# A cosine attention kernel: five score banks, wide exponentials, norms in the value banks and joint sums

## The chip, the cores and the metric

The kernel runs on one core of a Trainium2 chip. The metric is the device time of one execution in microseconds (us); lower is better. Five engines of the core work side by side, each through its own list of instructions in order: PE (matrix products), ACT (exponentials and other functions), DVE (vector work), POOL (vector work on the SBUF alone) and SP, which here only issues transfers. They wait for one another on semaphores.

## The reference

```python
Q_norm = Q / (np.linalg.norm(Q, axis=-1, keepdims=True) + 1e-10)
K_norm = K / (np.linalg.norm(K, axis=-1, keepdims=True) + 1e-10)
scores = np.einsum('bhqd,bhkd->bhqk', Q_norm, K_norm) / tau
weights = np.exp(scores - np.max(scores, axis=-1, keepdims=True))
weights = weights / (np.sum(weights, axis=-1, keepdims=True) + 1e-10)
return np.einsum('bhqk,bhkd->bhqd', weights, V).astype(np.float32)
```

Batch 8, 12 heads, sequence 512, width 64, tau 0.1, all in f32. Normalised scores are bounded, so the kernel takes no maximum.

## The kernel before, in words

The 96 heads are taken as 48 pairs (numbered 0 to 47; `s` in the code). A pair passes through these steps:

- **Load** (SP): Q, K and V of two heads, 256 KB each, into rings of buffers: `qk` (17 deep), `vf` (8). Each output goes out the same way from `ob` (8 deep), so the normalisation of pair s waits for the store of pair s-8.
- **Squares** (POOL, L368) into `sq`; **sums of squares**: K's on PE, as eight matmuls with the identity (`SSQ`, L385) that leave eight partial sums in columns 320 to 383 of a value bank, which DVE reduces (`RED`, L392); Q's by DVE straight from the SBUF (L396).
- **Norms**: eight small steps on DVE (`NEW`, L419 to L430), an inverse square root by a bit trick and two refinements, for a group of one, two or four pairs at a time. Its working values stand in `n_ps`, a PSUM bank of its own.
- **Scaling** to bf16 (`SCL`, L451): Q on DVE, K on POOL for most pairs. **Transposes** on PE (`TR`, L457), copied out by DVE (`EVA`, L465) into `qt`.
- **Scores** on PE (`SCO`, L551): a pair has eight tiles of 128 keys by 512 queries (four key blocks `c` by two heads `h`). One step of scores makes the two heads' tiles of a key block, in two of the four banks of `sc_ps`. The two heads lie in different halves of the rows.
- **Exponentials** on ACT (`EXP`, L567): one instruction of 1024 columns for both tiles, into `et` (five pairs deep). The next step of scores into these two banks waits for it. Pair 0 is done tile by tile (L543), the last block of pair 47 in three pieces (L562), and one block of pair 43 is done by a polynomial on DVE and POOL.
- **Values** on PE (`PV`, L587): sixteen matmuls for each head, into bank 0 or 1 of `o_ps`; then a reciprocal (`RCP`, L599) and a normalisation (`NRM`, L604) on DVE. A bank's next user waits for the normalisation, or for the reduction of the sums put there in between (`attached`).

Nothing is scheduled while it runs. `ORDER`, a table of numbers, sets each engine's list by hand, and the waits follow from each step's `needs`. Waits between two steps of PE, or of ACT, are left out, since those run in order.

The code picks the two banks for a key block's scores by turns:

```python
turn = chunks.index((s, c))
b = turn % 2
...
used = ... exps(*chunks[turn - 2])
P.add(("SCO", s, c), "pe", "sco", T0 + 0.9 * c, [("EVA", s)] + used, sco)
```

Of the kernel before, what the change touches and what calls it, by code (L numbers as in the profile page):

```python
# [108 lines left out]
def bass_cosine_similarity_attention_kernel(  # L109
# [26 lines left out]
    et = [sb(f"et{i}", [128, NT, 2, SEQ], bf16) for i in range(R_ET)]  # L136
# [13 lines left out]
    xw = sb("xw", [128, 2, SEQ], f32)  # L150

    sc_ps = nc.alloc_psum_tensor("scps", [128, 4, SEQ], f32)
# [5 lines left out]
    n_ps = nc.alloc_psum_tensor("nps", [128, R_X, MOST], f32)  # L158
# [34 lines left out]

    P.add("one", "pool", "one", -100, [], lambda e: e.memset(ones[:, :], 1.0))
# [23 lines left out]
    slots = sorted((START + PERIOD * (s + 1) + 0.9 * PV_AT[4 * h + 3] + 0.05 + late(s), s, h) for s in range(NP - 1) for h in range(2))  # L218
    chunks = [(s, c) for s in range(NP) for c in range(NT) if (s, c) not in OFF]
    off_of = {s: c for s, c in OFF}  # L220
    poly_groups = {group[s] for s in off_of}
# [4 lines left out]
    session, attached, early = {}, {}, []  # L226
    for s, w in sorted(((s, w) for s in range(NP) for w in range(2) if on_pe(s, w)), key=lambda j: (due_red(j[0]), j)):
        at = due_red(s) + 0.3
        if s < EARLY:
            early.append((s, w))  # L230
            continue
        due, i, h = next(x for x in slots if x[0] >= at and (x[1], x[2]) not in attached)
        attached[i, h] = (s, w)
        session[s, w] = (h, due, [("PV", i, h, NT - 1)])
    before = [[("EVA", 0, 1, 0), ("EVA", 0, 1, 1)], []]
    for s, w in sorted(early):
        b = w if s >= ONE_BANK else 0
        session[s, w] = (b, due_red(s), before[b])
        before[b] = [("RED", s, w)]
    bank_free = {}  # L240
    for s in range(NP):
        for h in range(2):
            bank_free[s, h] = before[h]
            before[h] = [("NRM", s, h)] + ([("RED",) + attached[s, h]] if (s, h) in attached else [])

    def head0(TF):
        for h in range(2):
# [10 lines left out]
            r_ps = sc_ps[:, 1, 0:4] if h == 0 else n_ps[:, 0, 0:4]  # L258
# [68 lines left out]

    def pair(s):
# [20 lines left out]
        red = [[("RED", 0, w, 0), ("RED", 0, w, 1)] if s == R_SQ else [key("RED", s - R_SQ, w)] for w in range(2)]  # L349
# [27 lines left out]
        for w in range(2):  # L377
            sqs = squares(s, w)
# [19 lines left out]
        xg, tg, yg = xs[g % R_X][:, 0 : 2 * m], ts[g % R_X][:, 0 : 2 * m], n_ps[:, g % R_X, 0 : 2 * m]  # L398
# [4 lines left out]
        reds = [("RED", i, w) for i in range(first[g], first[g] + sizes[g]) for w in range(2)]  # L403
# [14 lines left out]
        elif s == first[g]:  # L418
# [17 lines left out]
            for k in news(g):  # L436
                needs = [done] if k else reds + [("SCL", i, w) for i in past for w in range(2) if w == 0 or i in K_ON_DVE]
                if k == 0 and g == R_X:
# [3 lines left out]
                done = ("NEW", g, k)  # L442
                P.add(done, "dve", "new7" if k == 7 and on_dve else "new", TF - 4.9 - slack(s, M_NEW) + (M_STEP * (k - 7) if s > 8 else 0.23 * k), needs, steps[k])

        for w in range(2):
# [4 lines left out]
                  [("NEW", g, root(s, w))] + ([("TR", 0, w, 0), ("TR", 0, w, 1)] if s == R_QN else [key("TR", s - R_QN, w)]),  # L450
# [19 lines left out]
    def scos(s):  # L470
        if s < 0:
            return []
        if s in off_of:
            return [("SCO", s, c) if c != off_of[s] else ("SCX", s, c - c) for c in range(NT)] + [("SCX", s, 1)]
        return [("SCO", s, c) for c in range(NT)] if s else [("SCO", 0, c, h) for c in range(NT) for h in range(2)]

    def last_step(s, c):
        return 4

    def exps(s, c):  # L480
        if s < 0:
            return []
        if s == NP - 1 and c == NT - 1:
            return [("EXP", s, c, k) for k in range(3)]
        if s == 0:
            return [("EXP", s, c, h) for h in range(2)]
        return [("Y", s, last_step(s, c)) if (s, c) in OFF else ("EXP", s, c)]

    def poly(s, c, at):
# [3 lines left out]
        xp, xz = xps[len(prev) % 2], xzs[len(prev) % 2]  # L493
        done = lambda k: [("Y", prev[-k], last_step(prev[-k], off_of[prev[-k]]))] if len(prev) >= k else []
        a0, a1, a2, a3 = POLY
        for h in range(2):
            users = turn_user[turns[h]]
            before = [("X",) + users[users.index((s, h)) - 1] + (1,)] if users.index((s, h)) else []

            def sco(e, h=h):  # L500
                return e.matmul(out=x_ps, lhsT=qt[s % R_QT][64 * h : 64 * h + 64, 1, c, :],
                                rhs=qt[s % R_QT][64 * h : 64 * h + 64, 0, :, :], start=True, stop=True)

            P.add(("SCX", s, h), "pe", "sco1", at + h, [("EVA", s), ("EVA", turns[h])] + before, sco)
            P.add(("X", s, h, 0), "dve", "x1", at + h, [("SCX", s, h)] + done(2),
                  lambda e, h=h: e.tensor_scalar(out=xp[:, h, :], in0=x_ps, scalar1=BIG, scalar2=LIFT * UNIT - BIG, op0=ALU.add, op1=ALU.add))
            P.add(("X", s, h, 1), "dve", "x1", at + h, [("X", s, h, 0)],
                  lambda e, h=h: e.scalar_tensor_tensor(out=xz[:, h, :], in0=xp[:, h, :], scalar=a0 - LIFT * UNIT, in1=x_ps, op0=ALU.add, op1=ALU.subtract))
# [9 lines left out]
            ("dve", "ym", mul(e_, e_, p2))]  # L518
        for j, (eng, kind, step) in enumerate(steps):
            needs = [("Y", s, j - 1)] if j else [("X", s, h, 1) for h in range(2)]  # L520
            if j == 1:
                needs += done(1)
            if j == 3:
# [3 lines left out]
    def rest(s):  # L527
# [3 lines left out]
        for c in range(NT):  # L531
# [14 lines left out]
            turn = chunks.index((s, c))  # L546
            b = turn % 2

            def sco(e, c=c, b=b):
                for h in range(2):  # L550
                    last = e.matmul(  # L551
                        out=sc_ps[:, 2 * b + h, :], lhsT=qt[iqt][64 * h : 64 * h + 64, 1, c, :],
                        rhs=qt[iqt][64 * h : 64 * h + 64, 0, :, :], start=True, stop=True)
                return last

            used = [("EXP", 0, 2 * c + i, 1) for i in range(2)] if turn < NT + 2 else exps(*chunks[turn - 2])
            P.add(("SCO", s, c), "pe", "sco", T0 + 0.9 * c, [("EVA", s)] + used, sco)
            if last_pair and c == NT - 1:
                for k, (h, lo, hi) in enumerate(PIECES):
                    P.add(("EXP", s, c, k), "act", "exp1" if hi - lo == NT else "exph", T0 + 0.9 * c + 0.3 * k,  # L560
                          [("SCO", s, c)] + [key("PV", s - R_ET, i, NT - 1) for i in range(2)],
                          lambda e, c=c, b=b, h=h, q=slice(128 * lo, 128 * hi): e.activation(  # L562
                              out=et[iet][:, c, h, q], in_=sc_ps[:, 2 * b + h, q], func=ACT.Exp, scale=math.log(2.0) / UNIT if group[s] in poly_groups else inv_tau))
                continue
            P.add(("EXP", s, c), "act", "exp", T0 + 0.9 * c,
                  [("SCO", s, c)] + [key("PV", s - R_ET, h, NT - 1) for h in range(2)] + ["table"],
                  lambda e, c=c, b=b: e.activation(  # L567
                      out=et[iet][:, c, :, :], in_=sc_ps[:, 2 * b : 2 * b + 2, :],
                      func=ACT.Exp, scale=math.log(2.0) / UNIT if group[s] in poly_groups else inv_tau))
# [12 lines left out]
        for h in range(2):  # L582
            for i in range(NT):
                def pv(e, h=h, i=i):
                    for c in range(NT):
                        t = i
                        last = e.matmul(  # L587
                            out=o_ps[h][:, 65 * t : 65 * t + 65],
# [6 lines left out]
            grid = o_ps[h][:, 0 : 65 * NT].rearrange("p (t x) -> p t x", x=65)  # L595
# [230 lines left out]
```

## Time and profile before

| | |
|---|---|
| runs shown | 190.17, 193.73, 233.33 us; median 193.73 |
| profiled execution | span 189.6 us; its own whole time is not given, the quickest run is 190.17 |
| busy: PE, DVE, ACT, POOL | 175.8, 169.5, 182.2, 160.7 us |
| chain that ended last | ACT 73%, PE 8%, DMA 5%, POOL 5%, DVE 3% |
| transfers | 50.76 MB, mean 268 GB/s |

The span runs from the first to the last instruction of the program; the device time also holds what lies around it. A busy share is an average over the whole span. The chain is followed back from the last instruction, at each step to what released it, and says which engine's work set the end. Groups of instructions carry their line, engine and operation, then the tiles written and read, the shapes, the count, the busy time of the group and the mean time of one in ns. The mean is longer than busy time over count where one instruction begins before the record of the last one ends. A row of a window gives the busy time of each engine in that stretch.

### The profile page before, as it was taken

The numbers are of one execution on the slowest core, as the hardware profiler recorded it, in microseconds if no ns is written. First come the engines' busy times: TensorE is split into PE (matmuls) and PEld (weight loads), VectorE is DVE, ScalarE is ACT, GpSimd is POOL, SyncE is SP. The second block draws the span as 40 slices with busy tenths as digits, with TensorE's granted clock in tenths as the row PEclk, the third lists the DMA queues.
The fourth block names the chain that finished last, engine by engine and source line by source line (L and its number), as shares of the span: only waits on it lengthen the run. The fifth ranks groups of instructions, "written<-read, shape, count | busy, mean of one in ns | idle before, by whom it ended". The sixth has DMA issues, their size and how long they took to land.

```text
span 189.6 us, 6661 instructions
## 1 busy us (share of the span) xinstructions
PE 175.8 (93%) x2705; PEld 111.0 (59%) x2705; DVE 169.5 (89%) x541; ACT 182.2 (96%) x215; POOL 160.7 (85%) x149
## 2 busy tenths in 40 slices
PE   8798899999999999999899989999999899899992
PEld 2455456566665666666466656556666566555652
DVE  1779999999999999999899998999989999998752
ACT  5699999999999999999999999999999999999993
POOL 5599998999999999999999999999999994594000
PEclk9979999999999999999999999999999999999999
DMA  5999999998997898899999999996983062200655
GB/s 163 340 352 350 349 348 370 365 367 256 301 363 253 246 337 296 258 351 309 368 379 319 359 360 368 361 341 194 313 295 119 3 221 79 94 0 3 203 188 168
DMA packets 52446, 50.76 MB, mean 268 GB/s; under 512 B 3136, under 2 KB 52416, under 8 KB 52416
## 3 DMA queue, kind: packets, MB, share of 16 engines
q1 hardware_dynamic: 51984, 50.02, 80.1%
q8 instruction: 21, 0.34, 0.7%
q10 hardware_dynamic: 432, 0.33, 0.5%
q14 instruction: 9, 0.07, 0.1%
HBM read 37.75 MB, written 12.58 MB: 265 GB/s over the span
## 4 chain that ended last, share of the span: by engine, by line
ACT 73%; PE 8%; DMA 5%; POOL 5%; DVE 3%; SPq 2%; issue 1%; DVEq 0%
ACT et L567 73%; DMA out_dram<-ob 3%; DMA qk<-in_Q_dram 3%; PE ops L587 2%; PE scps L551 2%; POOL sq L368 2%; POOL vb L575 2%; POOL qn L451 2%; PE ops L385 1%; SPq L345 1%; PE tps L457 1%; PE scps L540 1%; DVE ob L604 1%; SPq L342 0%; PE ops L619 0%
## 5 line engine op out<-in xcount | busy, mean ns | idle before, releaser
L567 ACT ACTIVATE et<-scps 128x1024 bf16<-128x1024 f32 x186 | 170.9, 1182 | 0.7 <-PE scps L551 0.6
L368 POOL TENSOR_TENSOR sq<-qk 128x1024 bf16<-128x1024 f32 x44 | 82.6, 1893 | 0.2 <-DMA qk<-in_K_dram 0.2
L551 PE MATMUL scps<-qt 64*128 64x512 bf16 x374 | 73.0, 386 | 7.0 <-ACT et L567 4.1
L587 PE MATMUL ops<-vb,et 128*128 128x65 bf16 x1504 | 75.7, 195 | 1.0 <-DVE ob L604 0.6
L587 PEld LDWEIGHTS ops<-vb,et 128*128 128x128 bf16 x1504 | 57.3, 98 | 30.4 <-issue 18.4
L451 POOL TENSOR_TENSOR qn<-qk,rk 128x512 bf16<-128x512 f32 x38 | 39.2, 1042 | 7.1 <-DVE rk L426 7.0
L604 DVE TENSOR_TENSOR ob<-ops,rd 128x256 f32<-128x256 f32 x94 | 39.1, 420 | 1.5 <-DMA out_dram<-ob 0.8
L451 DVE TENSOR_TENSOR qn<-qk,nps 128x512 bf16<-128x512 f32 x56 | 36.9, 679 | 0.7 <-ACT nps L412 0.6
L465 DVE COPY qt<-tps 128x1024 bf16<-128x1024 bf16 x47 | 32.2, 684 | 0.8 <-PE tps L457 0.6
L457 PE MATMUL tps<-ident,qn 128*128 128x128 bf16 x376 | 32.3, 221 | 0.3 <-DVE qn L451 0.2
L551 PEld LDWEIGHTS scps<-qt 64*128 64x128 bf16 x374 | 18.4, 92 | 23.7 <-ACT et L567 8.3
L396 DVE TENSOR_REDUCE xs<-sq 128x8 f32<-128x512 bf16 x46 | 30.5, 673 | 0.2 <-POOL sq L368 0.2
L575 POOL TENSOR_SCALAR vb<-vf 128x512 bf16<-128x512 f32 x48 | 28.9, 619 | 0.0
L457 PEld LDWEIGHTS tps<-ident,qn 128*128 128x128 bf16 x376 | 21.8, 98 | 10.0 <-issue 5.0
L599 DVE RECIPROCAL rd<-ops 128x4 f32<-128x4 f32 x94 | 16.3, 176 | 5.0 <-PE ops L587 3.8
L385 PE MATMUL ops<-sq,ident 128*128 128x64 bf16 x384 | 19.5, 196 | 0.2 <-DVE qt L298 0.2
L385 PEld LDWEIGHTS ops<-sq,ident 128*128 128x128 bf16 x384 | 14.7, 99 | 4.3 <-issue 3.0
L392 DVE TENSOR_REDUCE xs<-ops 128x8 f32<-128x64 f32 x46 | 9.7, 210 | 0.8 <-PE ops L385 0.7
L419 DVE TENSOR_TENSOR ts<-xs,nps 128x32 f32<-128x32 f32 (+2 forms) x34 | 6.6, 194 | 0.6
L426 DVE SCALAR_TENSOR_TENSOR nps<-ts,nps 128x32 f32<-128x32 f32 (+3 forms) x34 | 6.7, 196 | 0.5
L422 DVE SCALAR_TENSOR_TENSOR ts<-ts,nps 128x32 f32<-128x32 f32 (+2 forms) x34 | 6.5, 192 | 0.4
L362 POOL TENSOR_TENSOR sq<-qk 128x512 bf16<-128x512 f32 (+1 forms) x5 | 4.7, 954 | 2.4 <-DMA qk<-in_K_dram 2.1
(60 smaller groups left out, 52.8 us busy)
## 6 DMA issues: line engine op xcount, KB each, us to landing
vf<-in_V_dram SPq DMA_DIRECT2D x48, 256.0 KB, 6.2
qk<-in_Q_dram SPq DMA_DIRECT2D x47, 256.0 KB, 5.2
qk<-in_K_dram SPq DMA_DIRECT2D x47, 256.0 KB, 6.2
out_dram<-ob SPq DMA_DIRECT2D x47, 256.0 KB, 5.7
qk<-in_Q_dram SPq DMA_DIRECT2D x2, 128.0 KB, 2.7
qk<-in_K_dram ACTq DMA_DIRECT2D x2, 128.0 KB, 2.9
out_dram<-ob SPq DMA_DIRECT2D x1, 128.0 KB, 1.7
out_dram<-ob ACTq DMA_DIRECT2D x1, 64.0 KB, 1.8
```

What stands on the lines that cost most here:

```text
L368: lambda e: e.tensor_tensor(out=sqf, in0=data, in1=data, op=ALU.mult))
L385: last = e.matmul(out=o_ps[bank][:, 320:384], lhsT=ident[:, :], rhs=sq[iqs][:, 8 * w : 8 * w + 8, 8 * k : 8 * k + 8], start=(k == 0), stop ...
L396: lambda e, w=w, dst=dst: e.tensor_reduce(out=dst, in_=sq[iqs][:, 8 * w : 8 * w + 8, :], axis=AX.X, op=ALU.add))
L451: lambda e, w=w, r=r: e.tensor_tensor(out=qn[iqn][:, w].rearrange("p t h d -> p h t d"), in0=qk[iq][:, w].rearrange("p h (t d) -> p h t d" ...
L457: last = e.transpose(t_ps[:, w, t, :], qn[iqn][:, w, t].rearrange("p h d -> p (h d)"), ident[:, :])
L465: lambda e: e.tensor_copy(out=qt[iqt][:, :, :, :].rearrange("p w t x -> p (w t x)"), in_=t_ps[:, :, :, :].rearrange("p w t x -> p (w t x)")))
L551: last = e.matmul(out=sc_ps[:, 2 * b + h, :], lhsT=qt[iqt][64 * h : 64 * h + 64, 1, c, :], rhs=qt[iqt][64 * h : 64 * h + 64, 0, :, :], sta ...
L567: lambda e, c=c, b=b: e.activation(out=et[iet][:, c, :, :], in_=sc_ps[:, 2 * b : 2 * b + 2, :], func=ACT.Exp, scale=math.log(2.0) / UNIT i ...
L575: lambda e: e.tensor_scalar(out=vb[:, ivb : ivb + n, :, :, 0:DIM].rearrange("p n h c d -> p (n h c) d"), in0=vf[:, iv : iv + n].rearrange( ...
L587: last = e.matmul(out=o_ps[h][:, 65 * t : 65 * t + 65], lhsT=et[iet][:, c, h, 128 * t : 128 * t + 128], rhs=vb[:, ivb, h, c, :], start=(c ...
L599: lambda e, h=h, grid=grid: e.reciprocal(out=rd[io][:, h, :], in_=grid[:, :, DIM]))
L604: lambda e, h=h, grid=grid: e.tensor_tensor(out=ob[io][:, h], in0=grid[:, :, 0:DIM], in1=rd[io][:, h, :].unsqueeze(2).to_broadcast([128, N ...
```

## The change

- `sc_ps` gets a fifth bank, in place of the bank that `n_ps` had. A new rule, `exp_groups`, cuts the run of score tiles from pair 8 on into units of three (banks 0 to 2) and two (banks 3 and 4) in turn; pairs 1 to 7 keep units of two in four banks. A unit may join two pairs, and is one step of scores and one exponential of 1536 or 1024 columns. There are 157 units where there were 187.
- The norms of groups 6 and later stand in the last 128 columns of value bank 1. Their steps, and scalings that read them on DVE, are tied to a window between the normalisation of one pair and the values of a later one (`in_window`): they wait for the `NRM`, and the first value matmul `PV` waits for them. The norms of groups up to 5 stand in the fifth score bank, which is unused until pair 8.
- Pairs 4 to 19 (`SUMMED_TOGETHER`) have Q's and K's sums of squares made together on PE (`together`): eight matmuls of 128 columns into value bank 0, and one reduction on DVE. All sums of later pairs go to bank 0 as well; Q's then stay with DVE. `BY_VECTOR`, the pairs whose K is summed by DVE, becomes 20 and 21 (was 43 and 47).
- Rings: `qk` 16 deep (17), `sq` 14 (16), the polynomial's `xw` twice. The last pair's third piece keeps its bank.
- All five lists of `ORDER` are written anew, SP's too.

```diff
-    sc_ps = nc.alloc_psum_tensor("scps", [128, 4, SEQ], f32)
+    sc_ps = nc.alloc_psum_tensor("scps", [128, 5, SEQ], f32)
...
-    n_ps = nc.alloc_psum_tensor("nps", [128, R_X, MOST], f32)
+    n_ps = both[:, :, 512 - 2 * MOST : 512].rearrange("p b (r x) -> p b r x", x=MOST)
+    n_head = sc_ps[:, 4, :].rearrange("p (r x) -> p r x", x=MOST)
...
+    def together(s, dst, g):
+        bank, due, before = session[s, 1]
+
+        def ssq(e):
+            for k in range(8):
+                last = e.matmul(
+                    out=o_ps[bank][:, 260:388], lhsT=ident[:, :], rhs=sq[s % R_SQ][:, :, 8 * k : 8 * k + 8],
+                    start=(k == 0), stop=(k == 7))
+            return last
+
+        P.add(("SSQ", s, 1), "pe", "ssqj", due, [*squares(s, 0), *squares(s, 1), "eye"] + before, ssq)
...
+    def in_window(key, w, b):
+
+        if w < 0:
+            window_ops.setdefault((0, b), []).append(key)
+            return [("RED", s, 1) for s in range(1, ONE_BANK)]
+        window_ops.setdefault((w + 1, b), []).append(key)
+        return [("NRM", w, b)]
...
+                if g > HEAD_GROUPS:
+                    needs = needs + in_window(done, max(first[g] - LEAD_STEP[k], summed_at.get(g, -1)), norm_bank(g))
...
+    def unit(u):
+        halves, bank = units[u]
...
+        def sco(e):
+            for i, (s, c, h) in enumerate(halves):
+                last = e.matmul(
+                    out=sc_ps[:, bank + i, :], lhsT=qt[s % R_QT][64 * h : 64 * h + 64, 1, c, :],
+                    rhs=qt[s % R_QT][64 * h : 64 * h + 64, 0, :, :], start=True, stop=True)
+            return last
...
+        P.add(("EXP", u), "act", {1: "exp1h", 2: "exp", 3: "exp3"}[n], T0, [("SCO", u), "table"] + free,
+              lambda e: e.activation(out=et_all[:, at : at + n, :], in_=sc_ps[:, bank : bank + n, :], func=ACT.Exp, scale=scale))
...
-            ends = lambda h: [("PV", s, h, NT - 1), ("SSQ",) + attached[s, h] if (s, h) in attached else None, key("NRM", s - R_O, h)]
+            ends = lambda h: [("PV", s, h, NT - 1), *[("SSQ",) + x for x in attached.get((s, h), [])[-1:]], key("NRM", s - R_O, h)]
...
+    for (s, b), keys in window_ops.items():
+        P.ops["PV", s, b, 0].needs += keys
...
-BY_VECTOR = (43, 47)
+BY_VECTOR = (20, 21)
...
-RINGS = (17, 8, 16, 6, 4, 4, 5, 8, 3)
+RINGS = (16, 8, 14, 6, 4, 4, 5, 8, 3)
...
+def exp_groups(NP, NT):
...
+                most = 2 if o or run[0][0] < FIRST_WIDE or run is runs[-1] else 3
+                for k in range(1, most + 1):
+                    if n + k <= len(run):
+                        cost = best[n, o][0] + (1 if k > 1 else 1.5)
```

What this moves, at three places. First PE's list while the scores of pairs 12 and 13 are made; `scps` are scores, `ops` values or sums, `tps` transposes. Before:

```order
L587 MATMUL ops<-vb,et 128x65 x12
L551 MATMUL scps<-qt 128x512 x2
L457 MATMUL tps<-ident,qn 128x128 x8
L587 MATMUL ops<-vb,et 128x65 x4
L551 MATMUL scps<-qt 128x512 x2
L587 MATMUL ops<-vb,et 128x65 x16
L551 MATMUL scps<-qt 128x512 x2
L385 MATMUL ops<-sq,ident 128x64 x8
```

The same engine and pairs after:

```order
L664 MATMUL ops<-vb,et 128x65 x16
L349 MATMUL ops<-sq,ident 128x128 x8
L550 MATMUL scps<-qt 128x512 x3
L507 MATMUL tps<-ident,qn 128x128 x8
L550 MATMUL scps<-qt 128x512 x2
L664 MATMUL ops<-vb,et 128x65 x20
L550 MATMUL scps<-qt 128x512 x3
L664 MATMUL ops<-vb,et 128x65 x8
L550 MATMUL scps<-qt 128x512 x2
```

Scores come in threes and twos, the sums are 128 columns wide (L349), and between two visits of scores stand up to twenty value matmuls.

Second DVE's list, where pair 9 is normalised (`ob<-ops,rd`). Before, Q's reductions from the SBUF (L396, `xs<-sq`) stand in it:

```order
L599 RECIPROCAL rd<-ops 128x4
L426 SCALAR_TENSOR_TENSOR rk<-ts,nps 128x16
L604 TENSOR_TENSOR ob<-ops,rd 128x256
L426 SCALAR_TENSOR_TENSOR nps<-ts,nps 128x16
L396 TENSOR_REDUCE xs<-sq 128x8
L451 TENSOR_TENSOR qn<-qk,nps 128x2x4x64
L599 RECIPROCAL rd<-ops 128x4
L396 TENSOR_REDUCE xs<-sq 128x8
L465 COPY qt<-tps 128x1024
```

After, with pair 9 normalised in the third row shown:

```order
L676 RECIPROCAL rd<-ops 128x4
L471 SCALAR_TENSOR_TENSOR ops<-ts,ops 128x32
L681 TENSOR_TENSOR ob<-ops,rd 128x256
L515 COPY qt<-tps 128x1024
L676 RECIPROCAL rd<-ops 128x4
L681 TENSOR_TENSOR ob<-ops,rd 128x256
L464 TENSOR_TENSOR ts<-xs,ops 128x32
L467 SCALAR_TENSOR_TENSOR ts<-ts,ops 128x32
L501 TENSOR_TENSOR qn<-qk,ops 128x2x4x64
```

The reductions from the SBUF are gone here, the two normalisations of the pair stand close together, and the norm steps work in `ops`, the value banks.

Third SP's list, from the loads of pair 9 on (`qk9` is the buffer of pair 9, `ob0` the output of pair 0; a `qk` number is that of the ring). Before:

```order
L342 DMA qk9<-in_Q_dram 128x2x256
L342 DMA qk9<-in_K_dram 128x2x256
L345 DMA vf<-in_V_dram 128x2x256
L342 DMA qk10<-in_Q_dram 128x2x256
L342 DMA qk10<-in_K_dram 128x2x256
L345 DMA vf<-in_V_dram 128x2x256
L342 DMA qk11<-in_K_dram 128x2x256
L342 DMA qk11<-in_Q_dram 128x2x256
L345 DMA vf<-in_V_dram 128x2x256 x3
L608 DMA out_0_dram<-ob0 128x2x256
```

After:

```order
L383 DMA qk10<-in_Q_dram 128x2x256
L383 DMA qk9<-in_Q_dram 128x2x256
L383 DMA qk9<-in_K_dram 128x2x256
L383 DMA qk10<-in_K_dram 128x2x256
L685 DMA out_0_dram<-ob0 128x2x256
L383 DMA qk11<-in_K_dram 128x2x256
L383 DMA qk0<-in_K_dram 128x2x256
L383 DMA qk12<-in_Q_dram 128x2x256
L383 DMA qk12<-in_K_dram 128x2x256
L383 DMA qk14<-in_K_dram 128x2x256
```

Q and K of one pair no longer stand together, loads of pairs far ahead (the second `qk0` is pair 16) come before nearer ones, V's loads move back, and the store of pair 0 moves up by seven places while those of pairs 1 to 3 move back by five to fifteen.

More of the change, by code (lines that the diff above doesn't have):

```diff
@@ L216, in due_red @@
         return due_sq(s) + 2.0
-    slots = sorted((START + PERIOD * (s + 1) + 0.9 * PV_AT[4 * h + 3] + 0.05 + late(s), s, h) for s in range(NP - 1) for h in range(2))
-    chunks = [(s, c) for s in range(NP) for c in range(NT) if (s, c) not in OFF]
+    units, unit_of = exp_groups(NP, NT)
     off_of = {s: c for s, c in OFF}
-    poly_groups = {group[s] for s in off_of}
+    poly_groups = {g for g in range(len(sizes)) if g not in NORM_ON_ACT} if off_of else set()
     turn_user = {}
@@ L437, in pair @@
                 needs = [done] if k else reds + [("SCL", i, w) for i in past for w in range(2) if w == 0 or i in K_ON_DVE]
+                if k == 0 and g > HEAD_GROUPS and slot_users[norm_bank(g)].index(g) >= 2:
+                    old = slot_users[norm_bank(g)][slot_users[norm_bank(g)].index(g) - 2]
+                    needs += [("SCL", i, w) for i in range(first[old], first[old] + sizes[old]) for w in range(2) if w == 0 or i in K_ON_DVE]
                 if k == 0 and g == R_X:
@@ L518, in poly @@
             ("dve", "ym", mul(e_, e_, p2))]
+        if s not in SEXTIC:
+            steps = [
+                ("pool", "ys", lambda e: e.tensor_scalar(out=w, in0=z, scalar1=a1, scalar2=a2, op0=ALU.add, op1=ALU.mult)),
+                ("pool", "yt", mul(w, w, z)),
+                ("dve", "yd", lambda e: e.scalar_tensor_tensor(out=e_, in0=w, scalar=a3, in1=z, op0=ALU.add, op1=ALU.mult)),
+                ("dve", "ym", mul(e_, e_, p2))]
         for j, (eng, kind, step) in enumerate(steps):
             needs = [("Y", s, j - 1)] if j else [("X", s, h, 1) for h in range(2)]
-            if j == 1:
-                needs += done(1)
-            if j == 3:
+            if j == (1 if s in SEXTIC else 0):
+                needs += done(2)
+            if j == len(steps) - 2:
                 needs += [key("PV", s - R_ET, h, NT - 1) for h in range(2)]
@@ L545, in rest @@
                 continue
[L546 to L569, printed above, removed]
+            for h in range(2):
+                if units[unit_of[s, c, h]][0][0] == (s, c, h):
+                    unit(unit_of[s, c, h])
         n = len(cast_with[s])
@@ L587, in pv @@
                         last = e.matmul(
-                            out=o_ps[h][:, 65 * t : 65 * t + 65],
+                            out=values[place(s, h)][:, 65 * t : 65 * t + 65],
                             lhsT=et[iet][:, c, h, 128 * t : 128 * t + 128], rhs=vb[:, ivb, h, c, :],
@@ L611, in last @@
         ivb, iet, io = s % R_VB, s % R_ET, s % R_O
-        spare = t_ps[:, :, :, :].rearrange("p w t x -> p (w t x)").bitcast(f32)
         for k, (h, lo, hi) in enumerate(PIECES):
-            bank = spare if k == 2 else o_ps[h]
+            bank = values[place(s, k)]
             for c in range(NT):
```

172 lines of the change are left out of this document (137 added, 35 removed), and 158 rows, old and new, of the table ORDER.

## The prediction

> **What bounds the kernel now.** I read the page first: its span, the busy time of each engine, and the chain that ended last by engine.
>
> ```profile
> span 189.6 us, 6661 instructions
> PE 175.8 (93%) x2705; PEld 111.0 (59%) x2705; DVE 169.5 (89%) x541; ACT 182.2 (96%) x215; POOL 160.7 (85%) x149
> ACT 73%; PE 8%; DMA 5%; POOL 5%; DVE 3%; SPq 2%; issue 1%; DVEq 0%
> ```
>
> Four engines are above 84%, so no share says by itself which one sets the end. The chain does: 73% of it is ACT. In order of time the chain runs along ACT twice, with a stretch between in which PE is as good a chain.
>
> ```profile
> 14.99 50.56 ACT et L567 x55
> ...
> 65.55 0.04 issue
> 65.59 0.39 PE scps L551 x2
> 65.98 0.04 issue
> 66.02 0.62 PE tps L457 x8
> 66.64 0.32 PE scps L551 x2
> 66.96 0.61 PE ops L587 x16
> 67.58 0.32 PE scps L551 x2
> 67.90 0.34 PE ops L385 x8
> 68.24 0.26 PE ops L587 x8
> ...
> 69.19 0.23 PE ops L385 x8
> ...
> 94.38 88.11 ACT et L567 x96
> ```
>
> An exponential of two tiles takes ACT 50.56 / 55 = 0.919 us (88.11 / 96 = 0.918). Did ACT ever wait? The view of waits for ACT names PE's scores (L551) as follows.
>
> ```profile
> ACT et L567 <- PE scps L551: 0.6, 2, 0.3
> ```
>
> So 0.6 us was lost in 186 exponentials. The steady part is bound by ACT, and two things can change the time: what one exponential costs, and whether PE still brings the scores in time. For the second, the stretches of the first third count.
>
> ```profile
> core 0: us, PE busy (x) PEld busy (x) DVE busy (x) ACT busy (x) POOL busy (x), PEclk, DMA share, GB/s
> 15.00:30.00 15.00, 13.34 (x212) 8.37 (x210) 14.44 (x53) 15.00 (x17) 13.54 (x13) 1.00 1.10 350
> 30.00:45.00 15.00, 14.44 (x233) 9.18 (x230) 14.73 (x52) 15.00 (x17) 14.92 (x14) 1.00 1.04 352
> 45.00:60.00 15.00, 14.52 (x241) 9.65 (x240) 14.84 (x52) 15.00 (x18) 15.00 (x15) 1.00 1.00 323
> ```
>
> PE has 1.66 + 0.56 + 0.48 = 2.7 us free in these 45; DVE has 1.0.
>
> **The wide exponentials.** Counted from the new planning rule, 186 exponentials of two tiles (and a last one in three pieces, as now) become 96 of two and 60 of three tiles. No row shows one of 1536 columns; what a third tile of 512 adds comes from groups by shape.
>
> ```profile
> L567 ACT ACTIVATE et<-scps 128x1024 bf16<-128x1024 f32 x186 | 170.9, 1182 | 0.7 <-PE scps L551 0.6
> L543 ACT ACTIVATE et<-scps,xa 128x512 bf16<-128x512 f32 x8 | 4.8, 683 | 0.0
> L562 ACT ACTIVATE et<-scps 128x256 bf16<-128x256 f32 x2 | 0.8, 575 | 0.0
> L562 ACT ACTIVATE et<-scps 128x512 bf16<-128x512 f32 x1 | 0.8, 768 | 0.0
> L360 ACT ACTIVATE sq<-qk 128x512 bf16<-128x512 f32 x1 | 0.6, 629 | 1.3 <-DMA qk<-in_Q_dram 1.3
> L360 ACT ACTIVATE sq<-qk 128x256 bf16<-128x256 f32 x1 | 0.4, 400 | 0.0
> ```
>
> From 512 to 1024 columns the same operation grows by 1182 - 768 = 414 ns, and the square grows by (629 - 400) x 2 = 458 ns per 512. Half of 0.918 is 0.459, at which a third tile would save nothing. The eight of L543 took 4.8 / 8 = 0.60 each, which leaves 0.918 - 0.60 = 0.32 as the other end (they carry a scale column, so this end is too low). I take 0.42, near the first figure, as it is the same operation. A wide one then takes 1.338 us in place of 1.5 x 0.918 = 1.377 and saves 0.039; sixty save **2.3 us**, between 0 and 60 x 0.139 = 8.3. The Trainium skill (ScalarE: Activation LUTs, What ACT_TABLE_LOAD costs) gives 0.833 ns per column and a fixed cost of which back-to-back instructions overlap a part; by its figure the third tile takes 0.427 and the gain is 60 x 0.032 = 1.9 us. The slope of 0.81 ns that the rows of L567 and L562 give agrees with it.
>
> **The joint sums on PE.** For pairs 4 to 19 the sums of squares of Q, which DVE reduced from the SBUF, join K's on PE: eight matmuls of 128 columns in place of eight of 64. The chain prices one pair on PE, each group to the start of the next: four visits of scores at 0.32, two lots of sixteen value matmuls at 0.61, transposes 0.62, sums 0.34, together 3.46 us. Eight matmuls of 128 columns are what the transposes are, 0.62 for eight, so a joint sum adds 0.28 us and sixteen add 4.5. They stand between the scores of pair 1 and of pair 14, where ACT will need 1.6 x (0.918 + 1.338) = 3.61 us a pair (eight tiles). With 16 sums in 13 pairs PE needs 3.46 - 0.34 + 0.62 x 16 / 13 = 3.88, which is 0.27 more than ACT, 3.5 us in all. Counted the other way, 4.5 of added work less the 2.7 us that PE has free leaves 1.8. Values may lag some pairs behind their exponentials (five buffers), so in the best case the overhang is put off and costs 0; in the worst none of the free time can be used and it costs 4.5. I take **+2.0 us**, near the 1.8 that rests on what PE did in this very stretch. What is late next is the score visit behind the sum in PE's queue, and with it ACT.
>
> **Scores in units of three and two.** A visit of three has a third matmul in a row half that the first still uses.
>
> ```profile
> 9.18 1.04 PE L540 MATMUL scps<-qt 64*128 64x512 bf16 x4
> ```
>
> Four single scores took 1.04 against 0.39 for a pair that starts together, (1.04 - 0.39) / 3 = 0.22 each; I add 0.22 for the third (0 if it could run beside the others, 0.39 if wholly alone). Five tiles then cost 0.32 + 0.54 = 0.86, before 2.5 x 0.32 = 0.80; half a change of kind less (the same eight sums take 0.34 or 0.23 by what stands beside them, so 0.11 for a change) gives 0.05 back. Net: nothing. But the margin moves. From the end of an exponential to the next start on ACT the chain shows 0.04 + 0.39 + 0.04 = 0.47 us, while ACT works for 0.918: 0.45 to spare. A unit of three needs 0.69 while ACT runs a unit of two: 0.23 to spare; the unit of two gets 0.87. PE's queue holds other groups of 0.23 to 0.62, so half the margin will be missed more often. Scaled from the 0.6 us of the 187 units now, twice the rate for sixty is **+0.4 us**; 0 is one end, the third rival below the other.
>
> **DVE, windows, transfers.** What DVE loses and what a window holds stands in these rows.
>
> ```profile
> L396 DVE TENSOR_REDUCE xs<-sq 128x8 f32<-128x512 bf16 x46 | 30.5, 673 | 0.2 <-POOL sq L368 0.2
> L392 DVE TENSOR_REDUCE xs<-ops 128x8 f32<-128x64 f32 x46 | 9.7, 210 | 0.8 <-PE ops L385 0.7
> ...
> 50.44 0.18 DVE L599 RECIPROCAL rd<-ops 128x4 f32<-128x4 f32 x1
> ...
> 50.65 0.42 DVE L604 TENSOR_TENSOR ob<-ops,rd 128x256 f32<-128x256 f32 x1
> ...
> 51.66 0.68 DVE L451 TENSOR_TENSOR qn<-qk,nps 128x512 bf16<-128x512 f32 x1
> ...
> 52.95 0.69 DVE L465 COPY qt<-tps 128x1024 bf16<-128x1024 bf16 x1
> ...
> 54.91 0.19 DVE L419 TENSOR_TENSOR ts<-xs,nps 128x32 f32<-128x32 f32 x1
> ```
>
> Sixteen reductions of 0.663 us (30.5 / 46) go, 10.6 us; the joint reduction reads 128 columns for 64 and adds up to 16 x 0.21 = 3.4. DVE is 3% of the chain, so I cost this at 0; it only helps PE wait less, at most the 1.0 us that DVE has free now, and it takes nothing off ACT. The norms now live in value bank 1, and PE's first value matmul of a pair there waits for up to four norm steps and a scaling; behind it on PE stand the pair's other values and the next scores, for which ACT waits. Such a window holds a reciprocal 0.18, a normalisation 0.42, four steps of 0.19, a scaling 0.68, and the 0.61 of values itself: 2.65 of 3.61 us. One transpose copy of 0.69 in DVE's queue still fits (3.34), a second doesn't. Value 0; if every window of forty pairs ran 0.1 over, 4 us. Bank 0's reciprocal waits for the longer sum, 0.28 later, in a window without norms: 0.
>
> SP's list is reordered: many loads of later pairs pass the stores of pairs 1 to 4. Each needs its `ob` buffer for the normalisation eight pairs on.
>
> ```profile
> out_dram<-ob SPq DMA_DIRECT2D x47, 256.0 KB, 5.7
> ...
> 45.62 0.47 SPq L345 DMA_DIRECT2D vf<-in_V_dram  x1
> ...
> 52.88 0.47 SPq L342 DMA_DIRECT2D qk<-in_K_dram  x1
> ...
> 57.70 0.42 DVE L604 TENSOR_TENSOR ob<-ops,rd 128x256 f32<-128x256 f32 x1
> ```
>
> The store of pair 1 now stands 60th of the single transfers. The 60th left at 45.62, so it lands at 51.3; pair 9 normalises at 50.65. The store of pair 3 stands 70th: 52.88 + 5.7 = 58.6 against 57.70. Both are just late on the old clock and just in time if pairs 9 to 11 run a microsecond later, as the joint sums make them. Cost 0, ends 0 and 2.
>
> **Sum.** 189.6 - 2.3 + 2.0 + 0.4 = 189.7 us of span. The quickest run shown, 190.17, lies 0.57 above the profiled span, which stands for what lies around it: **190.3 us**. The median of the three runs, 193.73, is 3.5 above that quickest run, and the third, 233.33, shows that it is not the program's own time; I forecast against 190.17. Within 2% means 186.4 to 194.0, about what a measurement of this kernel can tell from no change.
>
> **Rivals.**
> - *ACT keeps its rate.* PE's values lag and hide the sums: 189.6 - 2.3 + 0.57 = 187.9. For it: PE's 2.7 us free and the ring of five. Against it: the chain already passed through PE with 3.46 us a pair. Chance 0.25.
> - *Slower: the narrow margin is missed.* Where PE starts a lot of sixteen values (0.61) just as banks come free, the unit of three is 0.61 - 0.23 = 0.38 late. At a quarter of the sixty, 15 x 0.38 = 5.7 us comes in place of the 0.4: 195.6. It decides from about eleven such units on. Windows that overrun by 0.1 in forty pairs give nearly as much. For it: PE at 14.5 of 15 us; against it: 0.6 us of waiting in all now. Chance 0.18.
> - *The third tile costs its full 0.459.* The change then doesn't save what it says: 190.3 + 2.3 = 192.6. The square's row speaks for it. Chance 0.07.
> - *Stores come 2 us late* at pairs 9 to 12: 192.3. Chance 0.05.
>
> **How the numbers follow.** The forecast, 188.5 to 192.5 with the sums between 0.2 and 4.2, has 0.45. The floor, the full third tile and the late stores lie within 2% as well; of the missed margin nearly all is slower by more, with a little from sums at their worst: 0.20. Faster by over 2% needs a third tile of about 0.38 and PE in time, 0.06. That leaves 0.74 for within 2%. The range runs from just under the floor, 187.5, to the price of the missed margin, 195.6, and leaves out about 0.05 below and 0.13 above.
>
> **What would show it.** Exponentials of 1536 columns 1.30 to 1.38 us apart; ACT's waits for scores at 2 to 3 us, most of them before 70 us and ahead of three-tile units; PE above 14.6 of 15 us from 15 to 60; DVE with 2 us more room there. Waits of ACT spread evenly to the end would be the missed margin. DVE waiting for stores near 50 to 60 us would be the transfers. I am wrong if ACT waits under 1 us (the sums were hidden), or if wide exponentials take a step far from 1.34.

## The result, and the profile after

The changed kernel takes 191.47 us (median of 13 runs, 190.92 to 192.54) against 190.30 us for the kernel before (10 of its 13 runs): a ratio of **1.0062, 95% interval 1.0043 to 1.0080**. It is slower by 1.2 us, or 0.6%, which is small but clear of the noise. The forecast was 190.3, a time level with the quickest run of before that was known then (190.17). Here and in the table below, medians and ratios leave out runs over 1.5% above the quickest of the same kernel (for the kernel before 192.98, 193.73 and 233.33 us), and the trace of the last kernel of the table, taken in such a run of 207.0 us at a granted PE clock of 0.754 of full speed, is not read.

First the page of the changed kernel: span, busy time, and the chain that ended last by engine.

```profile
span 189.6 us, 6635 instructions
PE 177.1 (93%) x2705; PEld 109.7 (58%) x2705; DVE 167.2 (88%) x525; ACT 181.0 (95%) x185; POOL 160.7 (85%) x149
ACT 63%; PE 13%; POOL 9%; DMA 7%; issue 2%; DVE 2%; SPq 2%
```

ACT's share of the chain fell from 73% to 63%; PE rose from 8% to 13%, POOL and DMA together from 10% to 16%. The view of ACT's waits (in total, times, longest) says how much ACT lost, and that nearly all of it is one wait:

```profile
ACT et L579 <- PE scps L550: 2.2, 2, 2.1
```

The chain in order of time names the work behind it, and the timelines of POOL, PE and ACT each have their idle time in brackets:

```profile
31.68 7.72 DMA qk<-in_Q_dram
39.40 0.07 issue
39.47 2.23 POOL sq L409 x2
```

```profile
39.47 3.74 POOL L409 TENSOR_TENSOR sq<-qk 128x1024 bf16<-128x1024 f32 x2 [1.78 <-DMA qk<-in_Q_dram]
...
43.27 0.62 PE L349 MATMUL ops<-sq,ident 128*128 128x128 bf16 x8 [1.59 <-POOL sq L409]
...
44.85 3.71 ACT L579 ACTIVATE et<-scps 128x1536 bf16<-128x1536 f32 x3 [2.07 <-PE scps L550]
```

The load is Q of pair 14, the 46th transfer in SP's new list; six loads of Q and K of pairs 15 to 20 and the V loads of pairs 8 and 9, all needed later, go ahead of it. POOL stands at it for 1.78 us with pair 13's squares, whose loads had landed at 37.2, queued behind. The joint sum of pair 13 on PE waits for those squares, the scores queue behind the sum, and ACT loses 2.07 us.

The windows and the groups by shape answer to those of before:

```profile
15.00:30.00 15.00, 14.30 (x202) 9.08 (x200) 13.72 (x53) 14.79 (x17) 15.00 (x12) 1.00 1.10 355
30.00:45.00 15.00, 13.32 (x206) 8.63 (x203) 11.12 (x40) 12.93 (x15) 13.22 (x12) 1.00 1.10 349
45.00:60.00 15.00, 14.89 (x244) 9.94 (x244) 13.56 (x49) 14.65 (x13) 15.00 (x14) 1.00 1.04 348
```

```profile
L579 ACT ACTIVATE et<-scps 128x1024 bf16<-128x1024 f32 x96 | 96.5, 1053 | 0.2
L579 ACT ACTIVATE et<-scps 128x1536 bf16<-128x1536 f32 x60 | 88.4, 1474 | 2.4 <-PE scps L550 2.2
```

The middle window shows the stall on every engine: ACT 12.93, PE 13.32, DVE 11.12 of 15. In the windows around it DVE is at 13.7 and 13.6 where it was at 14.4 and 14.8. From start to start, a three-tile exponential takes 1.339 us (1.330 or 1.348) and a two-tile one 0.904 where nothing delays the next; with small delays the two-tile step averages 0.926 after 60 us, and 0.92 before the change.

**One table for all kernels.** The first microseconds differ from program to program (last section), so I also read from each trace when the exponentials had finished 18 tiles (the first step of pair 2), and the stretch from there to 380 tiles (the last full step of pair 47). The start and the stretch come from one traced execution of each kernel. The kernel before was run anew beside each set of kernels (medians from 190.0 to 190.5 us), and each ratio is to the runs beside it.

| kernel | 18 tiles at | stretch | median us | ratio to before, 95% |
|---|---|---|---|---|
| before | 18.76 | 166.47 | 190.30 | |
| changed | 17.61 | 167.62 | 191.47 | 1.0062 [1.0043, 1.0080] |
| one load moved | 17.78 | 166.10 | 190.54 | 0.9998 [0.9973, 1.0022] |
| squares swapped | 18.19 | 166.18 | 190.36 | 1.0002 [0.9981, 1.0022] |
| transfers by need | 18.50 | 165.27 | 189.92 | 0.9979 [0.9958, 1.0001] |
| the same again | 18.42 | 165.27 | 189.97 | 0.9980 [0.9958, 1.0002] |
| before, transfers by need | 17.17 | 166.56 | 190.28 | 0.9999 [0.9972, 1.0026] |
| by need, half sums | 20.34 | 165.25 | 190.87 | 1.0034 [1.0009, 1.0059] |
| the same again | 18.89 | 165.35 | 191.14 | 1.0041 [1.0012, 1.0069] |
| by need, double sums | 17.59 | 171.92 | 195.78 | 1.0326 [1.0282, 1.0371] |
| by need, own sums | 17.06 | 171.49 | 195.14 | 1.0262 [1.0227, 1.0296] |
| by need, two of three tiles | 18.48 | 164.04 | 189.17 | 0.9939 [0.9909, 0.9968] |
| by need, three tiles split | 17.65 | 168.76 | 192.96 | 1.0170 [1.0112, 1.0228] |
| by need, 23 scores ahead | 19.02 | 172.79 | 197.03 | 1.0344 [1.0306, 1.0382] |
| by need, two moves | 18.98 | 166.75 | 191.46 | 1.0036 [1.0004, 1.0069] |
| by need, twelve moves | not read | not read | 193.03 | 1.0119 [1.0068, 1.0169] |

The stretch of the changed kernel is 1.15 us longer than before's, which agrees with the 1.17 of the times.

### The profile page after: what moved, and what is told of

It reads as the page before. It is cut to its first block, busy times and chain, and to the rows that moved or that the text cites. A ratio compares the mean times of both kernels' runs of the same rounds, so it can differ in the third digit from the quotient of the medians.

```text
span 189.6 us, 6635 instructions
## 1 busy us (share of the span) xinstructions
PE 177.1 (93%) x2705; PEld 109.7 (58%) x2705; DVE 167.2 (88%) x525; ACT 181.0 (95%) x185; POOL 160.7 (85%) x149
## 4 chain that ended last, share of the span: by engine, by line
ACT 63%; PE 13%; POOL 9%; DMA 7%; issue 2%; DVE 2%; SPq 2%
ACT et L579 63%; DMA qk<-in_Q_dram 7%; PE ops L664 5%; PE scps L550 4%; POOL sq L409 4%; POOL vb L652 2%; POOL qn L501 2%; PE ops L349 2%; PE tps L507 1%; SPq L383 1%; POOL sq L403 1%; DVE ob L681 1%; SPq L380 0%; PE ops L695 0%; DVE ob L714 0%
## 5 line engine op out<-in xcount | busy, mean ns | idle before, releaser
L579 ACT ACTIVATE et<-scps 128x1024 bf16<-128x1024 f32 (+1 forms) x156 | 169.9, 1215 | 2.6 <-PE scps L550 2.2
L664 PE MATMUL ops<-vb,et 128*128 128x65 bf16 x1504 | 70.4, 195 | 0.2
L681 DVE TENSOR_TENSOR ob<-ops,rd 128x256 f32<-128x256 f32 x94 | 39.1, 420 | 1.5
L501 DVE TENSOR_TENSOR qn<-qk,ops 128x512 bf16<-128x512 f32 x46 | 31.1, 682 | 0.7
L550 PEld LDWEIGHTS scps<-qt 64*128 64x128 bf16 x374 | 16.2, 93 | 19.6 <-ACT et L579 4.0
L441 DVE TENSOR_REDUCE xs<-sq 128x8 f32<-128x512 bf16 x30 | 20.0, 673 | 0.3 <-POOL sq L409 0.3
L430 PE MATMUL ops<-sq,ident 128*128 128x64 bf16 x256 | 12.6, 193 | 0.2 <-DVE qt L314 0.2
L349 PE MATMUL ops<-sq,ident 128*128 128x128 bf16 x128 | 9.8, 219 | 2.1 <-POOL sq L409 2.1
L430 PEld LDWEIGHTS ops<-sq,ident 128*128 128x128 bf16 x256 | 9.5, 98 | 3.0 <-issue 1.8
L349 PEld LDWEIGHTS ops<-sq,ident 128*128 128x128 bf16 x128 | 7.4, 97 | 3.4 <-POOL sq L409 2.9
L501 DVE TENSOR_TENSOR qn<-qk,scps 128x512 bf16<-128x512 f32 x10 | 6.6, 682 | 0.7 <-ACT scps L457 0.6
L437 DVE TENSOR_REDUCE xs<-ops 128x8 f32<-128x64 f32 x30 | 6.2, 206 | 0.3
```

Source lines behind the costliest of these rows:

```text
L349: last = e.matmul(out=o_ps[bank][:, 260:388], lhsT=ident[:, :], rhs=sq[s % R_SQ][:, :, 8 * k : 8 * k + 8], start=(k == 0), stop=(k == 7))
L430: last = e.matmul(out=o_ps[bank][:, 320:384], lhsT=ident[:, :], rhs=sq[iqs][:, 8 * w : 8 * w + 8, 8 * k : 8 * k + 8], start=(k == 0), stop ...
L441: lambda e, w=w, dst=dst: e.tensor_reduce(out=dst, in_=sq[iqs][:, 8 * w : 8 * w + 8, :], axis=AX.X, op=ALU.add))
L501: lambda e, w=w, r=r: e.tensor_tensor(out=qn[iqn][:, w].rearrange("p t h d -> p h t d"), in0=qk[iq][:, w].rearrange("p h (t d) -> p h t d" ...
L550: last = e.matmul(out=sc_ps[:, bank + i, :], lhsT=qt[s % R_QT][64 * h : 64 * h + 64, 1, c, :], rhs=qt[s % R_QT][64 * h : 64 * h + 64, 0, : ...
L579: lambda e: e.activation(out=et_all[:, at : at + n, :], in_=sc_ps[:, bank : bank + n, :], func=ACT.Exp, scale=scale))
```

## Experiments: the transfers

**One load.** SP's list, by loads of Q and K:

```diff
 LD 12 Q
+LD 14 Q
 LD 12 K
 LD 14 K
 ...
 LD 20 K
-LD 14 Q
 LD 23 K
```

> The changed kernel with one transfer moved: the load of Q of pair 14, 46th in SP's list, becomes 34th. Theory T (a late transfer is the price of the change): POOL's wait of 1.8 us for this load, and with it ACT's wait of 2.1 us for scores at 42.8, go; 191.5 becomes 189.2 to 189.7, a ratio of 0.993 to 0.996 to the kernel before. Theory S (PE's joint sums are the price, as the prediction had it): the 2 us are lost ahead of other scores instead, and the time stays at 191.0 to 191.6.

Measured: 190.54 us. ACT's waits and POOL's timeline in its trace:

```profile
ACT et L579 <- PE scps L550: 0.6, 2, 0.4
```

```profile
36.27 5.60 POOL L409 TENSOR_TENSOR sq<-qk 128x1024 bf16<-128x1024 f32 x3
```

POOL does its three squares without a break and ACT's wait falls from 2.2 to 0.6. Of these 0.6, 0.4 stand where the 2.07 were, so the late load itself had cost about 1.6. The stretch falls by 1.52 us and the time by 0.93 (1.2 by the ratios), less than theory T had: the range of 189.2 to 189.7 was missed, and the kernel stands level with before. Theory S is refuted: what was lost at the load was not lost again at other scores.

**Squares swapped.** POOL's list:

```diff
-SQ 14
 SQ 13
+SQ 14
```

> The changed kernel, SP's list as in it; only POOL makes the squares of pair 13 (whose loads land at 37.2 us) ahead of those of pair 14 (39.4). If the 2.1 us of ACT come from POOL standing at a late load, with pair 13's joint sum and the scores behind it on PE, this frees as much as moving the load did: 190.3 to 190.8. If the loads' order harms in other ways too, it stays at 191.2 or more.

Measured: 190.36 us, inside the first range, and a stretch of 166.18. SP's list is as in the changed kernel and the load still lands late (at 40.0 us); only pair 13's squares no longer stand behind it. So the price lies in POOL's order meeting SP's, and either list can be mended. Both orders are the change's own: in the kernel before POOL squares pair 13 ahead of pair 14, and Q of pair 14 is the 42nd transfer.

**All transfers by need.** The rule: of the transfers whose buffer is free, the one whose data are used first in the changed kernel's trace.

> The changed kernel with SP's whole list sorted by when each transfer is first needed (and no sooner than its buffer is free). Theory T: as with the one load moved, 189.2 to 189.7, since only that load made an engine on the chain wait; no engine but POOL at the start waits for a load. Theory S: 191.0 to 191.6, with ACT still waiting 2 us for scores between 20 and 60 us.

Measured: 189.92 us, and 189.97 in the run below; the stretch is 165.27. That is 2.35 us less than the changed kernel's, somewhat more than the wait of 2.07; half a microsecond of the difference to the one moved load lies before the 26th tile, where this kernel started later. The time again misses the range of theory T, by 0.2. It is quicker than the changed kernel by 1.5 us, and 0.2% below before, with both intervals just touching 1.

> The same kernel as the list by need, once more, beside the other two: 189.6 to 190.3 if its time does not hang on the loading of the program, with the stretch at 165.2 to 165.8 us.

**The kernel before, by need.**

> The kernel before with SP's list sorted by need by the same rule. Theory T: its transfers made ACT wait nowhere, so it stays within 0.3 us of 190.5. A rival, that SP's list costs the kernel before as much as the changed one: it falls by 1 us or more, and the list by need says nothing of the change.

Measured: 190.28 us, stretch 166.56 against 166.47: on balance its own list cost it nothing. In detail it did cost something. With its own list one normalisation waits for a store, and at 92 us a step of scores comes 0.6 us late behind it:

```profile
DVE ob L604 <- DMA out_dram<-ob: 0.8, 1, 0.8
```

By need this wait is gone, but a step at 37 us comes 0.6 us late, behind a scaling that POOL finished late. The rule gains on balance only where the changed kernel's list had lost.

Like against like, with the transfers of both kernels by need, the change shortens the stretch by 1.29 us (166.56 to 165.27). The medians are only 0.36 us apart (190.28 and 189.92); in the traced executions the changed kernel's exponentials start 1.33 us later (18.50 against 17.17).

## Experiments: the joint sums on PE and DVE

**Half and double.** Four, and sixteen, matmuls of 128 columns for a joint sum:

```diff
-            for k in range(8):
+            for k in range(4):
...
-                    start=(k == 0), stop=(k == 7))
+                    start=(k == 0), stop=(k == 3))
```

> As the list by need, but a joint sum makes four matmuls of 128 columns in place of eight; it leaves out half of the squares. PE does about 16 x 0.28 = 4.5 us less. Theory T with PE just fitting: ACT waits under 0.6 us less than with the list by need, time 188.8 to 189.5. Theory S: PE had no room for the joint sums, and the time falls by 1 to 2 us against the list by need.

> The same kernel as the list by need with half of each joint sum (half of the squares left out), once more. Its stretch was as with the list by need (165.25 against 165.27 us) but its time was 190.87 against 189.92. If that came from the start, which differs from one loading of a program to the next, the time now is 189.5 to 190.3 with the same stretch; if half the sums do cost time somewhere, 190.7 to 191.1 again.

> The list by need with sixteen matmuls of 128 columns for a joint sum in place of eight (each square is counted twice), 4.5 us more on PE before 60 us. The steady stretch, from the 18th tile of exponentials to the 380th, took 165.27 us with the list by need and 165.25 with half the sums. Theory T2 (the joint sums stood in room that PE had): under 1 us more, 165.3 to 166.3. Theory S2 (the sums as made fill PE to the brim, PE being at 14.8 to 15.0 of 15 us from 15 to 60): most of the 4.5 us shows, 168 to 170 us in the stretch and 2 to 4 us in the time.

Half the sums: stretch 165.25 and 165.35 against 165.27. The 4.5 us that the prediction charged to PE are worth nothing as they stand. The times were nevertheless 190.87 and 191.14, so my reading that a loading of the program explains them is wrong: in both loadings the program loses time outside the stretch. It starts later both times (ACT's wait for Q of pair 1, half sums first, list by need second):

```profile
ACT sq L401 <- DMA qk<-in_Q_dram: 1.9, 1, 1.9
```

```profile
ACT sq L401 <- DMA qk<-in_Q_dram: 1.1, 1, 1.1
```

That wait ends before the first joint sum. The larger part comes at the end: from the 380th tile to the end of the span the two traces with half sums take 5.6 and 5.7 us, and the other traces that were read 4.3 to 4.8. SP takes longer to issue the last two stores, 1.44 and 1.58 us for both together against 0.82 (list by need first, half sums second):

```profile
185.49 0.82 SPq L718 DMA_DIRECT2D out_dram<-ob  x2
```

```profile
187.32 1.44 SPq L718 DMA_DIRECT2D out_dram<-ob  x2
```

Why this program's first loads land later, and its last store is issued more slowly, was not found.

Double sums: 195.78 us, a stretch of 171.92, above both ranges, which is 6.65 more for 4.5 us of work. Waits of ACT and DVE:

```profile
ACT et L579 <- PE scps L550: 5.7, 15, 0.9
...
DVE xs L356 <- PE ops L349: 3.9, 7, 1.1
```

So PE was filled to the brim by the sums, as its windows with transfers by need show (14.80, 14.91 and 14.99 of 15):

```profile
15.00:30.00 15.00, 14.80 (x206) 9.42 (x205) 14.32 (x54) 14.91 (x17) 15.00 (x13) 1.00 1.10 350
30.00:45.00 15.00, 14.91 (x244) 10.27 (x243) 12.57 (x46) 14.59 (x16) 15.00 (x14) 1.00 1.09 367
45.00:60.00 15.00, 14.99 (x235) 9.62 (x233) 13.84 (x51) 14.81 (x15) 15.00 (x14) 1.00 1.09 380
```

With half the sums they read 13.92, 14.60 and 14.16 (the second loading). The first 4.5 us fitted, the next cost more than their length. A doubled sum also holds value bank 0 for longer, for which DVE waits; the two effects were not told apart.

**The joint sums undone.**

```diff
-SUMMED_TOGETHER = (4, 5, 6, ..., 19)
+SUMMED_TOGETHER = ()
```

> The list by need with the joint sums undone: for pairs 4 to 19 PE sums K's squares alone (eight matmuls of 64 columns) and DVE reduces Q's from the SBUF again, just ahead of K's reduction; 16 x 0.66 = 10.6 us more on DVE and 4.5 less on PE. If DVE's relief is worth nothing (the prediction cost it at 0): 165.3 to 166 us for the steady stretch, the time within 0.7 us of the list by need. If wide exponentials and norm windows in the value banks need the room that DVE got (45 - 40.7 = 4.3 us free from 15 to 60): DVE overflows by about 5 us there, the stretch takes 168 to 171 and the time 192.5 to 195.

Measured: 195.14 us, stretch 171.49, 6.2 more, a little above the second ranges. The chain of this kernel, and two of PE's waits:

```profile
ACT 57%; DVE 29%; PE 11%; issue 2%
```

```profile
PE ops L664 <- DVE ops L471: 2.5, 5, 0.6
...
PE ops L664 <- DVE ob L681: 2.0, 5, 0.6
```

The wide exponentials with norms in a value bank need the room that the joint sums gave DVE: PE's values wait for norm steps (L471) and normalisations (L681). Q's reductions were put back at one fixed place, ahead of K's, with the rest of the lists unchanged; a list planned anew for this kernel might lose less.

## Experiments: ACT and the order on PE

**Less work on ACT.** The third tile is left out of each wide exponential:

```diff
-... out=et_all[:, at : at + n, :], in_=sc_ps[:, bank : bank + n, :], ...
+... out=et_all[:, at : at + min(n, 2), :], in_=sc_ps[:, bank : bank + min(n, 2), :], ...
```

> The list by need, the exponentials of three tiles reading and writing only the first two (the third tile's exponentials are left out); ACT does up to 60 x 0.43 = 26 us less. What the other engines need shows: if ACT alone bounds the kernel from pair 8 on, the time falls until the next engine binds, PE at 177 us of busy time, to 178 to 182 us. If PE is as much the bound as ACT, it falls under 4 us, to 186 to 189.

Measured: 189.17 us, a stretch of 164.04. Some 26 us less on ACT by steps (17 by its busy time) bring 1.2 in the stretch. The chain passes to PE and DVE, and ACT now waits 48 times:

```profile
PE 50%; DVE 26%; POOL 15%; issue 3%; DMA 3%; ACT 2%; SPq 0%
```

```profile
ACT et L579 <- PE scps L550: 14.8, 48, 0.6
```

**More work on ACT.** Each wide exponential in two instructions:

```diff
-lambda e: e.activation(out=et_all[:, at : at + n, :], ...)
+lambda e: [e.activation(out=et_all[:, at + i : at + j, :], ...)
+           for i, j in ((0, min(n, 2)), (2, n)) if i < j][-1]
```

> The list by need, each of the sixty exponentials of three tiles issued as one of two tiles and one of one tile, in place, with the same waits. A step of three tiles took 1.340 us; 0.904 (two tiles, undisturbed) and 0.48 (one tile, the step of the 512-column piece at the end) make 1.384, 60 x 0.044 = 2.6 us more on ACT. If ACT's time counts in full, although 26 us less of it gave only 1.2 (theory T3: ACT and PE stand at the same level, so less of one gains little and more of either costs), the stretch grows from 165.3 to 167.3 to 168.2 us and the time to 191.9 to 192.8. If PE alone sets the pace, it grows by under 1 us.

```profile
L579 ACT ACTIVATE et<-scps 128x1024 bf16<-128x1024 f32 x156 | 155.0, 1090 | 0.5 <-PE scps L550 0.4
L579 ACT ACTIVATE et<-scps 128x512 bf16<-128x512 f32 x60 | 39.9, 665 | 0.0
```

Measured: 192.96 us, stretch 168.76, 3.5 more. From start to start the two parts took 0.913 and 0.477 us, 1.390 together, so 60 x 0.050 = 3.0 was added. The kernel exceeded the range, but theory T3 holds: ACT's time counts in full when it grows and hardly when it shrinks.

**Scores ahead on PE.** Three kernels move steps of scores that were late for ACT ahead in PE's list, for example past pair 13's sum:

```diff
+SCO 32
 SSQ 13
 PV 6 (three groups of four matmuls)
-SCO 32
```

> The list by need; in PE's list 23 of the 157 steps of scores, those that came 0.03 to 0.56 us late for ACT in its trace (2.6 us in all, 27 late steps), move ahead of the one to four groups before them. If these small delays are the rest of what PE costs ACT and PE has room to do the passed work a little later, the stretch from the 18th to the 380th tile falls from 165.3 to 163.0 to 164.0 us and the time by 1 to 2 us, to 188 to 189. If PE is full (theory S2, borne out by the doubled sums), the passed groups come late instead and the stretch stays at 165 to 166.

> The list by need with two steps of scores moved ahead on PE: the one that made ACT wait 0.56 us (past the joint sum of pair 13 and three groups of four value matmuls of pair 6) and the one of 0.29 us (past the joint sum of pair 15). If these were mere order, the stretch falls by 0.5 to 0.9 us, to 164.4 to 164.8, and the time to 189.1 to 189.5. If what is passed is needed at once by DVE or POOL (PE full), the stretch stays at 165.3 or grows to 166.

> The list by need with twelve steps of scores, 0.03 to 0.12 us late each (0.7 us in all), moved ahead of one group of four value matmuls (0.13 us). If the loss of the 23 moves came from those past sums and transposes, the stretch falls by 0.3 to 0.7 us, to 164.6 to 165.0. If any delay of values costs, since a bank's normalisation and the norm steps behind it start later, it grows by 1 to 4 us.

All three got slower: 197.03, 191.46 and 193.03 us. The stretches of the first two, 172.79 and 166.75, lie above both of the ranges that were given; the times of the third agree with its second reading. Waits with the list by need, then with 23 steps ahead, then with two:

```profile
DVE rd L676 <- PE ops L664: 3.3, 9, 0.7
...
ACT et L579 <- PE scps L550: 0.9, 3, 0.4
```

```profile
DVE rd L676 <- PE ops L664: 6.5, 14, 0.9
...
ACT et L579 <- PE scps L550: 5.3, 11, 1.3
```

```profile
ACT et L579 <- PE scps L550: 2.1, 2, 1.3
```

With 23 moves ACT's waits grow from 0.9 us to 5.3 and DVE's for values from 3.3 to 6.5; with two, ACT's longest wait is 1.3 us where it was 0.4. The passed values end later, and DVE, which also has little room, starts the normalisation later; the norm steps in the window behind it, the scaling and a later pair's scores would follow. The rise of DVE's wait is measured; the rest of that path is argued. That twelve moves past one group of values also cost 3.1 us against the list by need (2.7 by the ratios) shows that the passed sums and transposes were not needed for a loss.

## Why the prediction was wrong, point by point

- **The number.** The span was forecast as 189.7 and came out as 189.6, but this is luck, and the step from span to time was wrong. I set the span of the one profiled execution (189.6) beside the quickest time (190.17) and took 0.57 us for what lies around a span. It is 1.87 for the changed kernel (191.47 - 189.6), and in 35 further executions of before it was 1.8 to 2.1. The profiled execution of before was thus one of about 191.5 us, 1.2 above the median: it reached 18 tiles 1.15 us later than the changed kernel's did, and that hid the 1.15 us by which the changed kernel's stretch is longer. With 1.9 in the sum, the 189.7 would have become 191.6; and against the median of before, the sum should have started from a span of about 188.4. As a change, the sum said +0.1 us, and +1.2 was measured.
- **Transfers: cost 0, ends 0 and 2. This is the step that failed.** I looked at stores passed by loads, and neither at loads passed by loads nor at the order of POOL's squares behind them. The price was 2.07 us of ACT's wait, through POOL's squares, of which 0.4 remains with the load moved; moving one load or swapping two squares took 0.9 to 1.1 us of the time back, the whole list by need 1.5. The rival at 0.05, "stores come 2 us late", had the size and the wrong transfer: no normalisation of the changed kernel waited for a store.
- **Joint sums: +2.0. Wrong too.** Halving them left the stretch where it was. What remains between the 26th and the 100th tile with transfers by need is 0.73 us over before (34.67 against 33.94) but 0.11 over before by need (34.56), and halving the sums gives back 0.06 to 0.17 of it. Two late steps of scores, 0.56 and 0.29 us, stand where the units of three begin, each behind a joint sum on PE; with half the sums the first shrinks to 0.34 and the second goes, but others come late instead. The first rival's reason, that PE's values hide the sums, was right; but the room was just used up, as the doubled sums show. That the total still came near is luck: the 2.0 charged to the sums is about what the late load cost.
- **Wide exponentials: -2.3, with +0.4 for the margin. The sign was right, the net of -1.9 somewhat too large.** A three-tile step is 1.339, forecast 1.338. From the 100th to the 380th tile the changed kernel takes 126.94 us and before 128.86, 1.9 us more; but before loses about 0.5 there to the store that came late, and before by need takes 128.33. So the exponentials gained about 1.4. Against the undisturbed step of 0.904 the third tile costs 0.435, and 60 x (1.356 - 1.339) gives only 1.0; my 0.918 had small delays in it that I counted as the exponential's own time. By the Trainium skill (ScalarE: Activation LUTs, What ACT_TABLE_LOAD costs) a third tile is estimated at 0.427; the 0.435 measured here is 2% more. The lengths from 26 to 380 tiles differ by +0.8 between changed and before: -1.9 in the later part, +0.7 in the beginning of the wide units, and +2.0 by which the transfers by need shorten that beginning.
- **DVE's relief: 0.** Whether it gains anything by itself was not tried, but it is what the rest stands on: without it 6.2 us are lost.
- **"The steady part is bound by ACT": half the truth.** 73% of the chain and 0.6 us of waiting in 186 exponentials looked like one bound. In the changed kernel 26 us less on ACT bring 1.2: with these lists PE and DVE stand at the same level, so a saving on ACT alone is worth little more. Whether other lists could use it was not tried.
- **The rivals.** "ACT keeps its rate" asked for 187.9; with transfers by need the kernel does 189.9. The missed margin (waits spread evenly to the end) did not come: after 60 us ACT shows no wait for scores in the windows (15.00 of 15). "I am wrong if ACT waits under 1 us" came true once the load was mended (0.9), which says that the sums were hidden. Of the signs named, "ACT's waits at 2 to 3 us, most of them before 70 us and ahead of three-tile units" held to the letter (2.2, at 44.85), for a reason I had not given: a sign that several causes share tells none of them. PE above 14.6 us from 15 to 60 came only with the transfers mended (14.80, 14.91, 14.99; in the changed kernel 14.30, 13.32, 14.89). DVE had 5.6 us more room from 15 to 60 (44.0 to 38.4 busy, partly the stall), 3.3 with the transfers mended; 2 was forecast.

## What to carry to other kernels

When a list of transfers is reordered, go through every load and compare its place in the queue with the first instruction that needs it, and with what stands behind that instruction on its engine; one load twelve places late cost here about what the new exponentials had gained. A chain that lies 73% on one engine says who was last, not how far the others are behind: a kernel with that engine's work cut down shows it in one run. A span and a time may only be set side by side from the same execution. And when two kernels differ by a microsecond, split the time into start, stretch and end first: with half sums nearly the whole difference lay outside the part that was edited.

## What the runs showed of the hardware

- The same first six loads land at different times in different programs, and at like times in two loadings of one (one traced execution each): Q of pair 1 at 6.46 and 6.57 us with the list by need, at 7.33 and 7.11 with half sums, and at 5.50 in the kernel before by need. The exponentials shift with it, and the stretch began at 17.06 to 20.34 us. What in a program sets it stayed open.
- The granted clock of PE goes with the start as well. In the traced execution of before it stood at half of full speed for 3.4 us (PEclk 0.87 from 5 to 10 us and 0.79 from 10 to 15); in that of the changed kernel it stayed at 1.00. The six read traces with such a spell of 3.4 us reached 18 tiles at 18.42 to 18.98, the one with 6.8 us (half sums, first loading) at 20.34, and those without at 17.06 to 18.19, but for one at 19.02 (23 scores ahead). Of 105 further executions of before, the 76 with a mean clock of 0.995 or more have a median of 190.05 us, the 29 with 0.991 or less 191.31. How much of this is the clock and how much the late loads that go with it was not separated.
- With SP's queue full, a transfer of 256 KB lands 7 to 8 us after its issue (7.72 for the late one) and, in the changed kernel from 30 to 46 us, the landings are about 0.75 us apart, so a place in the list is worth about 0.75 us there.
- A three-tile exponential takes one of two steps, 1.330 or 1.348 us, in about equal numbers; what decides between them was not tried.
